# Five more projections with each hi weight tile run over hi and lo of the operand in one product

## The chip, the cores and the metric

The kernel runs on one core of a Trainium2 chip. The metric is the time of one execution on the device, in microseconds; of several runs the median counts. TensorE, the matrix engine, multiplies a stationary tile of weights (128x128) with a moving operand and adds into PSUM, which has eight banks of 128 partitions by 512 float32 columns. ScalarE (ACT) and VectorE (DVE) are the elementwise engines; both read PSUM. Weights come from HBM by DMA.

## The reference, cut to what matters

Two blocks on x with 256 tokens and 2048 features, batch 1, float32.

```python
# first block: RG-LRU
proj = rmsnorm(x, norm_pre) @ a_w_in            # 2048 -> 2 x 2048: xb and gate
xc   = causal_conv4(xb) + b;  r, i = sigmoid(blockwise(xc))
h    = scan(a(r), sqrt(1 - a^2) * i * xc);  y = (h * silu(gate)) @ a_w_out
x    = x + rmsnorm(y);  x = x + sigmoid(x @ ple_w_gate) * (p @ ple_w_proj)
# second block: one input projection, three branches
h = rmsnorm(x, g0)
u_pool, u_conv, c_gate, b_gate, q, k, v, q_idx, k_idx, w_idx = split(h @ w_in)
y_pool = (window_mean(u_pool) - u_pool) @ pool_w         # four window widths
y_conv = b_gate * causal_conv3(c_gate * u_conv)
y_attn = softmax over the 64 keys with the best index score (q_idx, k_idx, w_idx)
x = x + rmsnorm((sum of sigmoid(h @ w_gate) * (y @ w_branch)) @ w_out)
x = x + rmsnorm(square(relu(rmsnorm(x) @ w_up)) @ w_down)
```

The products are wanted to float32 accuracy. The kernel writes each operand as hi + lo, hi being rounded to 12 significant bits, and adds hi\*hi + hi\*lo + lo\*hi.

## The kernel before

**Layout and stream.** Features lie on the partitions and tokens on the free axis, so a product is a 128x128 tile of weights against 256 columns of the operand. All weights pass once, in the order of their use, through one stream (class `Stream`): a DMA on SP's queue brings a chunk (three buffers), ACT rounds it to hi (L88), DVE subtracts to lo (L99), in pieces of up to 1024 columns, that is, eight weight tiles (six in the conv projection). Five pieces are split ahead. `pumped` (L395), called after the products of each piece, emits the split of a later piece, whose buffer is that of the piece just multiplied; so on ACT each rounding waits until TensorE is done with that piece, and what is emitted behind it on ACT waits as well.

**Two forms of product.** `Group` (L344) holds four output tiles in two PSUM banks and makes three products of 256 columns per weight tile (L358): hi over the operand's hi, hi over its lo, lo over its hi. `Wide` (L367) gives each output tile a whole bank. The hi weights run once over 512 columns, hi and lo of the operand side by side (L378), into the two halves of the bank; the lo weights run over 256 columns into the left half (L379). The halves must be added at the evacuation: `merged` (L382) copies the right halves to SBUF on ACT (L387), one instruction per tile, and adds the left halves on DVE (L391), one per tile, and then the banks are free. Before the change `Wide` serves the ple gate, the branch gates, two branch products, most of w_out, and the MLP.

**The order beside the products** is set by `Sched`. A task (engine, cost in us, what it depends on, buffers it takes and frees) waits in one list, in order of creation. At each `pump`, once per piece, the list is walked in that order, and a task is emitted if its engine has room, its dependencies were emitted earlier (by at least one piece if on another engine, three for a TensorE task), and its buffers are free. DVE's room grows per eight-tile piece by 8 x 0.3275 - 1.13 = 1.49 us. Engines execute in order of emission. `make_room` (L165) is the way out when a new group needs banks that are not free: it takes the first task in the list that frees a bank and emits it at once, with all that it depends on, whatever the room. Freed banks are handed out again in the order in which they were freed. Large SBUF tiles of 128x4x256 are tagged T4, with ten buffers.

**Where the changed projections stand.** Block 1 runs, for m = 0 to 3, an xb group and a gate group of a_in (16 k-tiles by 4 tiles each), and between them, for m from 1 on, the recurrence gates `ri` of an earlier m: two `Group`s of one piece each. The sums of the first norm (`rstd`, L524) are wanted by every evacuation of a_in and are made during m = 1: a bank, tiny products (L532), a root on ACT (L545), five small DVE steps, a transposing product (L559). Then come a_w_out (three `Group`s open together) and the ple products. Block 2 projects key index, query index, key and query (`att_group`, 19 tiles), with v and the index weights (`vb`, two banks) after the third group; 16 index scores (`dots`, one bank each, L1020) run beside the query groups, the top-k on DVE (L1047) beside the first pool group, the relative bias goes through DRAM (L1085), then pool (two groups) and conv (eight groups of three tiles); attention's small products run beside the conv groups.

Of the kernel before, what the change touches and what calls it, by code (L numbers as in the profile page):

```python
"""RG-LRU block followed by a three-branch (pool / conv / sparse attention) block.

Everything on chip is laid out [feature on partitions, token on the free axis].
Every float32 product runs on the tensor engine as three float32r passes: an
operand v is split exactly into hi = round(v) (12 significant bits) and
lo = v - hi, and v*w = hi*hi + hi*lo + lo*hi.
"""
# [16 lines left out]
P = 128  # L24
T = 256
# [10 lines left out]
# columns of the packed per-feature vectors  # L36
# [12 lines left out]
class Stream:  # L49
    """The weights in the order of their use: loaded, split into hi and lo, handed out in pieces."""  # L50
# [28 lines left out]
    def split_hi(self):  # L79
        """Rounds one more piece; says how much of a full piece it was."""  # L80
        i = self.hi_done
        if i >= len(self.pieces):
            return 0.0
        _, _, w, src = self.piece(i)
        hi = self.pool.tile([P, 1024], F32R, tag="whi", bufs=self.hl_bufs, name=f"whi{i}")
        lo = self.pool.tile([P, 1024], F32R, tag="wlo", bufs=self.hl_bufs, name=f"wlo{i}")
        self.hl[i] = (hi[:, :w], lo[:, :w])
        self.nc.scalar.activation(hi[:, :w], src, AF.Copy)  # L88
        self.hi_done += 1
        return w / 1024  # L90

    def split_lo(self):
        """What the rounding of one more piece left."""
        i = self.lo_done
        if i >= self.hi_done:
            return 0.0
        c, last, w, src = self.piece(i)
        hi, lo = self.hl[i]
        self.nc.vector.tensor_tensor(lo, src, hi.bitcast(F32), op=ALU.subtract)  # L99
        self.lo_done += 1  # L100
        if last:
            del self.raw[c]
            self.load()
        return w / 1024
# [5 lines left out]
    def split_first(self, parts):  # L110
        """The first piece bit by bit, as it comes in."""
# [27 lines left out]
class Sched:  # L139
    """Spreads the work beside the matrix products over the pieces of the weight stream.  # L140

    A task is emitted once its engine has room in the current piece, the buffers that it takes
    are free, and what it depends on was emitted far enough ahead that no engine waits."""
# [3 lines left out]
    def __init__(self, bufs):  # L147
        self.q, self.now = [], 0
        self.room = {"ACT": 0.0, "DVE": 0.0, "POOL": 0.0, "PE": 0.0}
        self.left = dict(bufs)  # L150

# [13 lines left out]
    def make_room(self, **tags):  # L165
        """Emits tasks ahead of their turn until so many buffers are free."""
        for tag, n in tags.items():
            while self.left[tag] < n:
                self.need(next(t for t in self.q if tag in t.free))

    def emit(self, t):
        self.q.remove(t)
        self.make_room(**t.take)
        t.fn()
# [34 lines left out]
def tile_kernel(ctx: ExitStack, tc: tile.TileContext, d):  # L209
# [115 lines left out]
    def table(fn):  # L325
        """Brings the table of fn in before it is waited for."""
        act.activation(small(1, "tbl"), one, fn)
# [3 lines left out]
    # products of zeros keep TensorE at its full clock while it waits  # L331
# [12 lines left out]
    class Group:  # L344
        """Output tiles accumulated side by side, two to a PSUM bank."""
# [21 lines left out]
    class Wide:  # L367
        """Output tiles of one bank each: hi weights run over hi and lo of the operand side by side,
        into the two halves of the bank, which are added when the bank is evacuated."""
# [12 lines left out]
        def merged(self, box, name, *deps):  # L382
            """Tasks that leave the sum in box[name], a new tile."""
# [17 lines left out]
    def linear(grp, kts, rhs, pieces, last_kt, before=None):  # L401
        """Pieces of the stream, each [kt][tile] of 128 columns, into the group's tiles."""
# [22 lines left out]
    def full_by_bank(grp, rhs, evac, n=KT):  # L425
        """As full, but the first bank is finished, and evacuated, ahead of the second."""
# [26 lines left out]
    def q4(h, n):  # L453
        """hi and lo of four tiles"""
# [8 lines left out]
    def split_tasks(get, *deps, free=None):  # L463
        """get() -> hi, lo, source; the hi and lo of four tiles"""
# [10 lines left out]
    def scaled_tasks(h, k0, src, gname, *deps):  # L475
        """hi and lo of src * g, g per feature, for four tiles"""
# [12 lines left out]

    class Norm:  # L490
        """Sum of squares over the features and the reciprocal root of its mean."""
# [19 lines left out]
        def tasks(self, srcs, *deps):  # L511
            """Adds the squares of four tiles, in one or two parts."""
# [11 lines left out]
        def rstd(self, extra=(), wait=True, fill=(), idle=(0, 0)):  # L524
            """Tasks that leave in .r, [128, T], 1 / sqrt(mean + eps) in every partition, and by
            token in .c, [128, 2]; emitted at once where the next product waits for them."""
# [55 lines left out]
    # =====================================================================  # L582
    # block 1: RG-LRU
    # =====================================================================
# [24 lines left out]
    # softplus(-lam) = max(-lam, 0) + log1p(exp(-|lam|)),  log1p(e) = 2 atanh(e / (2 + e))  # L609
# [39 lines left out]

    def xb_done(m, grp):  # L650
        box = {}

        def scale():
            box["xb"], box["xc"] = t4(n="xb"), t4(n="xc")
            scale_banks(box["xb"], grp, n0.r)
# [18 lines left out]
        sc = Dv(1.2, scale, r_done[0], take=T4[2], free=PS[2])  # L674
# [5 lines left out]
    def g_done(m, grp):  # L680
        box = {}

        def scale():
            box["g"] = t4(n="g")
            scale_banks(box["g"], grp, n0.r)
# [8 lines left out]
        box["done"] = Dv(1.13, silu, A(0.95, sig, Dv(1.2, scale, r_done[0], take=T4[1], free=PS[2]), take=T4[1]),  # L694
# [3 lines left out]
    def ri(m):  # L698
# [19 lines left out]
        # with L = 8 r softplus(-lam), t = tanh(L / 2), a = exp(-L):  # L718
        # 1 - a = (1 + a) t  and  1 - a^2 = (1 + a)^2 t
# [43 lines left out]
    for m in range(4):  # L763
        grp = Group(4)
# [14 lines left out]
        grp = Group(4)  # L779
# [20 lines left out]
    def out_last(rhs, fill=(None, None), idle=(0, 0)):  # L800
        """The last four tiles, which the next product waits for; fill: products meanwhile."""
# [41 lines left out]
    # per-layer embedding: p @ ple_w_proj meanwhile  # L843
# [26 lines left out]
    # x += y * rstd, and its hi and lo, four tiles at a time  # L870
# [58 lines left out]
    # =====================================================================  # L929
    # block 2  # L930
    # =====================================================================
# [26 lines left out]
    att_ready = {}  # L958

    def att_group(i0, n):  # L960
        g = Group(n)
# [5 lines left out]
        def evac(m):  # L967
            dve.tensor_tensor(att_dst(i0 + m), g.ps(m), n2.r, op=ALU.mult)

        for m in range(n):  # L970
            att_ready[i0 + m] = Dv(0.35, lambda m=m: evac(m), r2_done[0], take=T4[1],
                                   free=PS[(n + 1) // 2 if m == n - 1 else 0])
# [5 lines left out]
    # v and wi with the tokens on partitions  # L978
# [26 lines left out]
    v_ready = A(0.9, v_done, att_ready[9], take=T4[1])  # L1005
    wi_ready = Dv(0.3, wi_done, v_ready, free=PS[2])

# [56 lines left out]
    # relative bias as a Toeplitz band: query q, key k reads rel[h, 127 - q + k].  One copy of rel  # L1064
    # per query lies in DRAM; reading it with a pitch one short of a copy shifts it by one per query.
# [149 lines left out]
    YS = hl16("YS")          # pool branch in tiles 0..7, conv branch in tiles 8..15  # L1215
    dhl, d_ready = {}, {}

    def pool_done(grp, n):
        box = {}

        def scale():
            box["u"], box["s"], box["q"] = t4(n="pu"), t4(n="pws"), t4(n="pq")
            scale_banks(box["u"], grp, n2.r)
# [24 lines left out]
        s = Dv(1.2, scale, take=T4[3], free=PS[2])  # L1248
# [4 lines left out]
    for n in range(2):  # L1253
        g = Group(4)
# [35 lines left out]
    def conv_done(m, grp):  # L1290
        box = {}

        def scale():
            box["uc"], box["z"] = t2(n="uc"), t1("z")
            dve.tensor_tensor(box["uc"], grp.banks[0], bc(n2.r, 2), op=ALU.mult)
            dve.tensor_tensor(box["z"], box["uc"][:, 0, :], box["uc"][:, 1, :], op=ALU.mult)
            S.free(T2=1)
# [12 lines left out]
        def gate():  # L1310
            dve.tensor_tensor(box["z"], grp.ps(2), n2.r, op=ALU.mult)
            dve.tensor_tensor(box["y"], box["y"], box["z"], op=ALU.mult)
# [7 lines left out]
        z = Dv(1.0, scale, take=dict(T2=1, T1=1))  # L1320
        y = Dv(0.8, taps, A(0.4, tap2, z, take=dict(T1=1)))
        y = Dv(0.7, gate, y, free=dict(ps=2, T1=1))
# [3 lines left out]
    for m in range(8):  # L1326
        g = Group(3)
# [215 lines left out]

def _kchunks(w, groups, kper=4):
    """w [K, M] -> [group, K / (kper * 128)][128][kper * len(group) * 128]: groups of column tiles."""
# [13 lines left out]
def _featT(a):  # L1559
    """[tokens, F] -> [128, F / 128, tokens]"""  # L1560
# [15 lines left out]
def _pack(i):  # L1576
# [15 lines left out]
    ri = np.concatenate([i["a_w_r"][0], i["a_w_i"][0]], axis=2)          # [8, 256, 512]  # L1592
# [3 lines left out]
    w = i["ple_w_proj"][0].reshape(2, P, 2, 2, 512).transpose(2, 1, 3, 0, 4)   # [chunk, p, grp, kt, 512]  # L1596
# [50 lines left out]
```

## Time and profile before

| | |
|---|---|
| median of 3 runs | 2001.24 us (1999.24, 2001.24, 2011.94) |
| span of the profiled execution | 2012.2 us |
| TensorE busy | 1984.8 us (99%), 13097 products |
| weight loads of TensorE | 1811.0 us (90%) |
| VectorE busy | 1274.3 us (63%) |
| ScalarE busy | 1001.4 us (50%) |
| DMA | 366 MB, 182 GB/s on average |
| chain that ended last | TensorE 96%: L378 40%, L358 33%, L379 20% |

A busy time on TensorE is the union of overlapping records: one 256-column product is recorded as 0.28 us, but the next one starts long before it ends. What a product costs the stream is the distance from its start to the next start.

### The profile page before, as it was taken

How to read it: one execution, taken by the hardware profiler on the slowest of the kernel's cores; microseconds unless marked ns; L12 is line 12 of the kernel's file. 1: busy time of each engine (PE TensorE's matmuls, PEld its weight loads, DVE VectorE, ACT ScalarE, POOL GpSimd, SP SyncE). 2: the span in 40 equal slices, each digit the busy share in tenths (PEclk: the TensorE clock that was granted, in tenths of full speed). 3: DMA queues.
4: the chain of work that ended last, by engine and by line, in shares of the span. 5: the costliest groups of instructions: out<-in, count | busy, mean ns of one | idle time of the engine just before them, and what ended most of it. 6: DMA issues, size and time to landing. Idle time of an engine off the chain costs nothing.

```text
span 2012.2 us, 31390 instructions
## 1 busy us (share of the span) xinstructions
PE 1984.8 (99%) x13097; PEld 1811.0 (90%) x13097; DVE 1274.3 (63%) x1642; ACT 1001.4 (50%) x1317; POOL 0.3 (0%) x6
## 2 busy tenths in 40 slices
PE   9999999999999999999999999999999999999996
PEld 8999999899999998888889989788888888888886
DVE  6788857765577776565656555865555556555665
ACT  6576755653434445454544455554444345434552
POOL 0000000000000000000000000000000000000000
PEclk9999999999999999999999999999999999999998
DMA  7545454554356455555555555455555555555552
GB/s 279 178 177 187 173 206 175 188 189 172 131 157 205 159 196 190 184 183 184 185 187 187 189 189 189 147 183 184 184 185 188 187 189 188 189 187 183 184 181 82
DMA packets 55846, 366.12 MB, mean 182 GB/s; under 512 B 6008, under 2 KB 8344, under 8 KB 16280
## 3 DMA queue, kind: packets, MB, share of 16 engines
q1 hardware_dynamic: 53424, 361.18, 51.6%
q10 hardware_dynamic: 2280, 2.93, 0.8%
q8 instruction: 102, 1.67, 0.3%
q14 instruction: 40, 0.33, 0.0%
HBM read 360.42 MB, written 3.67 MB: 181 GB/s over the span
## 4 chain that ended last, share of the span: by engine, by line
PE 96%; DVE 2%; DMA 1%; ACT 0%; issue 0%; SPq 0%; DVEq 0%; ACTq 0%
PE ps L378 40%; PE ps L358 33%; PE ps L379 20%; DMA wraw<-in_conv_in 1%; PE ps L1020 0%; DVE wlo L99 0%; DMA wraw<-in_a_in 0%; PE ps L1117 0%; DVE m L1529 0%; PE ps L532 0%; DVE X L1538 0%; PE ps L989 0%; PE ps L990 0%; PE ps L991 0%; DVE X L826 0%
## 5 line engine op out<-in xcount | busy, mean ns | idle before, releaser
L99 DVE TENSOR_TENSOR wlo<-wraw,whi 128x1024 fp32r<-128x1024 f32 (+2 forms) x701 | 831.1, 1190 | 663.3 <-ACT whi L88 662.4
L88 ACT ACTIVATE whi<-wraw 128x1024 fp32r<-128x1024 f32 (+2 forms) x701 | 721.6, 1032 | 934.8 <-PE ps L378 613.6
L378 PE MATMUL ps<-N,whi 128*128 128x512 f32 x1024 | 363.9, 400 | 3.5 <-DVE N L472 3.5
L378 PE MATMUL ps<-HD,whi 128*128 128x512 f32 x960 | 339.4, 399 | 0.0
L358 PE MATMUL ps<-G,whi 128*128 128x256 f32 x1632 | 300.2, 286 | 0.2 <-ACT whi L88 0.2
L379 PE MATMUL ps<-N,wlo 128*128 128x256 f32 x1024 | 288.2, 281 | 0.0
L378 PE MATMUL ps<-G,whi 128*128 128x512 f32 x768 | 271.0, 397 | 0.0
L379 PE MATMUL ps<-HD,wlo 128*128 128x256 f32 x960 | 269.6, 281 | 0.0
L358 PEld LDWEIGHTS ps<-G,whi 128*128 128x128 f32 x1632 | 256.4, 193 | 3.0 <-issue 0.6
L378 PEld LDWEIGHTS ps<-N,whi 128*128 128x128 f32 x1024 | 193.1, 189 | 52.6 <-DVE N L472 3.0
L358 PE MATMUL ps<-G,wlo 128*128 128x256 f32 x816 | 232.2, 285 | 3.4 <-DVE wlo L99 3.4
L378 PEld LDWEIGHTS ps<-HD,whi 128*128 128x128 f32 x960 | 180.4, 188 | 45.1
L379 PE MATMUL ps<-G,wlo 128*128 128x256 f32 x768 | 215.6, 281 | 0.0
L379 PEld LDWEIGHTS ps<-N,wlo 128*128 128x128 f32 x1024 | 194.2, 190 | 0.0
L358 PE MATMUL ps<-U,whi 128*128 128x256 f32 x1024 | 187.9, 286 | 1.8 <-ACT whi L118 1.6
L379 PEld LDWEIGHTS ps<-HD,wlo 128*128 128x128 f32 x960 | 181.3, 189 | 0.0
L378 PEld LDWEIGHTS ps<-G,whi 128*128 128x128 f32 x768 | 144.2, 188 | 35.2
L358 PEld LDWEIGHTS ps<-U,whi 128*128 128x128 f32 x1024 | 161.8, 194 | 3.2 <-ACT whi L118 2.2
L358 PEld LDWEIGHTS ps<-G,wlo 128*128 128x128 f32 x816 | 157.7, 193 | 3.8 <-DVE wlo L99 3.8
L358 PE MATMUL ps<-U,wlo 128*128 128x256 f32 x512 | 146.2, 286 | 0.2 <-DVE wlo L119 0.2
L379 PEld LDWEIGHTS ps<-G,wlo 128*128 128x128 f32 x768 | 145.1, 189 | 0.0
L358 PEld LDWEIGHTS ps<-U,wlo 128*128 128x128 f32 x512 | 99.4, 194 | 0.4 <-DVE wlo L119 0.4
(257 smaller groups left out, 2412.7 us busy)
## 6 DMA issues: line engine op xcount, KB each, us to landing
wraw<-in_up SPq DMA_DIRECT2D x64, 1024.0 KB, 4.8
wraw<-in_down SPq DMA_DIRECT2D x64, 1024.0 KB, 4.8
wraw<-in_gate SPq DMA_DIRECT2D x48, 1024.0 KB, 4.7
wraw<-in_a_in SPq DMA_DIRECT2D x29, 1024.0 KB, 4.8
wraw<-in_conv_in SPq DMA_DIRECT2D x32, 768.0 KB, 4.4
wraw<-in_branch SPq DMA_DIRECT2D x24, 1024.0 KB, 4.8
wraw<-in_a_out SPq DMA_DIRECT2D x16, 1024.0 KB, 4.8
wraw<-in_ple_gate SPq DMA_DIRECT2D x16, 1024.0 KB, 4.8
```

Of the source, the lines that this page charges most:

```text
L88: self.nc.scalar.activation(hi[:, :w], src, AF.Copy)
L99: self.nc.vector.tensor_tensor(lo, src, hi.bitcast(F32), op=ALU.subtract)
L358: pe.matmul(self.ps(m), lhsT, rhs, start=b not in self.begun, stop=stop, skip_group_check=True)
L378: pe.matmul(self.banks[m], wh, xhl, start=m not in self.begun, stop=False, skip_group_check=True)
L379: pe.matmul(self.banks[m][:, 0, :], wl, xhl[:, 0, :], start=False, stop=stop, skip_group_check=True)
```

## The change

The groups of a_in other than the first two, all `att_group`s, the pool groups and the conv groups become `Wide`. Their evacuations read the merged sum in SBUF and scale it there. In the att groups each tile has its own three tasks (copy, add, scale). The conv evacuation takes its tile from T4 in place of T2 and scales three tiles at once. `make_room` now skips tasks that wait for a task which is itself being emitted. All else in the diff is comments taken out.

```diff
     def make_room(self, **tags):
         for tag, n in tags.items():
             while self.left[tag] < n:
-                self.need(next(t for t in self.q if tag in t.free))
+                self.need(next(t for t in self.q if t.free.get(tag, 0) > 0 and self.clear(t)))
+
+    def clear(self, t):
+        return all(x.done is not None or (x not in self.busy and self.clear(x)) for x in t.deps)
...
+    def scale_tiles(box, name, grp, r):
+        if isinstance(grp, Wide):
+            dve.tensor_tensor(box[name], box[name], bc(r, 4), op=ALU.mult)
+        else:
+            box[name] = t4(n=name)
+            scale_banks(box[name], grp, r)
...
+    def scale_task(grp, box, name, scale, more):
+        if isinstance(grp, Wide):
+            return Dv(1.2, scale, r_done[0], grp.merged(box, name), take=T4[more])
+        return Dv(1.2, scale, r_done[0], take=T4[1 + more], free=PS[2])
...
-        sc = Dv(1.2, scale, r_done[0], take=T4[2], free=PS[2])
+        sc = scale_task(grp, box, "xb", scale, 1)
...
     for m in range(4):
-        grp = Group(4)
+        grp = Wide(4) if m else Group(4)
         if m == 0:
             grp_g = Group(4)
...
         if m > 1:
             ri(m - 1)
-        grp = Group(4)
+        grp = Wide(4)
         full(grp, rhsU)
         g_done(m, grp)
...
     def att_group(i0, n):
-        g = Group(n)
+        g = Wide(n)
         full(g, rhsG)
...
-        def evac(m):
-            dve.tensor_tensor(att_dst(i0 + m), g.ps(m), n2.r, op=ALU.mult)
+        def right(m):
+            act.activation(att_dst(i0 + m), g.banks[m][:, 1, :], AF.Copy)
+
+        def left(m):
+            dve.tensor_tensor(att_dst(i0 + m), att_dst(i0 + m), g.banks[m][:, 0, :], op=ALU.add)
+
+        def scale(m):
+            dve.tensor_tensor(att_dst(i0 + m), att_dst(i0 + m), n2.r, op=ALU.mult)
 
         for m in range(n):
-            att_ready[i0 + m] = Dv(0.35, lambda m=m: evac(m), r2_done[0], take=T4[1],
-                                   free=PS[(n + 1) // 2 if m == n - 1 else 0])
+            l = Dv(0.35, lambda m=m: left(m), A(0.4, lambda m=m: right(m), take=T4[1 if i0 + m in NEW else 0]),
+                   free=PS[1])
+            att_ready[i0 + m] = Dv(0.3, lambda m=m: scale(m), l, r2_done[0])
...
-        s = Dv(1.2, scale, take=T4[3], free=PS[2])
+        s = Dv(1.2, scale, grp.merged(box, "u"), take=T4[2])
...
     for n in range(2):
-        g = Group(4)
+        g = Wide(4)
         full(g, rhsG)
         pool_done(g, n)
...
-            dve.tensor_tensor(box["uc"], grp.banks[0], bc(n2.r, 2), op=ALU.mult)
+            dve.tensor_tensor(box["uc"][:, :3, :], box["uc"][:, :3, :], bc(n2.r, 3), op=ALU.mult)
...
-        z = Dv(1.0, scale, take=dict(T2=1, T1=1))
+        z = Dv(1.2, scale, grp.merged(box, "uc"), take=dict(T1=1))
         y = Dv(0.8, taps, A(0.4, tap2, z, take=dict(T1=1)))
-        y = Dv(0.7, gate, y, free=dict(ps=2, T1=1))
+        y = Dv(0.35, gate, y, free=dict(T4=1, T1=1))
...
     for m in range(8):
-        g = Group(3)
+        g = Wide(3)
         full(g, rhsG)
```

## Rows read from the trace of the kernel before

**Rows 1.** Busy times by stretch: length, PE, PEld, DVE, ACT, POOL, PEclk, DMA, GB/s
```profile
56.00:312.00 256.00, 256.00 (x2139) 256.00 (x2138) 193.28 (x245) 166.05 (x223) 0.00 (x0) 1.00 0.52 183
550.00:596.00 46.00, 46.00 (x380) 45.22 (x379) 38.34 (x89) 17.57 (x19) 0.00 (x0) 1.00 0.52 156
596.00:760.00 164.00, 160.44 (x1292) 159.00 (x1291) 119.05 (x196) 74.98 (x114) 0.00 (x0) 0.98 0.55 179
```

**Rows 2.** What PE waited for: us in total, times, longest us
```profile
PE ps L378 <- DVE N L472: 3.5, 2, 2.4
```

**Rows 3.** Timeline of PE in block 1, form of three products: start, us
```profile
199.85 0.40 PE L358 MATMUL ps<-U,whi 128*128 128x256 f32 x2
...
200.21 0.40 PE L358 MATMUL ps<-U,whi 128*128 128x256 f32 x2
```

**Rows 4.** Timeline of PE in the branch gates, wide form over G
```profile
999.83 0.40 PE L378 MATMUL ps<-G,whi 128*128 128x512 f32 x1
...
1000.89 0.40 PE L378 MATMUL ps<-G,whi 128*128 128x512 f32 x1
```

**Rows 5.** Timeline of PE in the ple gate, wide form over H
```profile
369.67 0.39 PE L378 MATMUL ps<-H,whi 128*128 128x512 f32 x1
...
371.75 0.39 PE L378 MATMUL ps<-H,whi 128*128 128x512 f32 x1
```

**Rows 6.** Timeline of ACT: in brackets the idle time before, and its releaser
```profile
71.77 1.06 ACT L88 ACTIVATE whi<-wraw 128x1024 fp32r<-128x1024 f32 x1 [1.82 <-PE ps L358]
...
514.70 0.84 ACT L88 ACTIVATE whi<-wraw 128x768 fp32r<-128x768 f32 x1 [2.68 <-PE ps L358]
515.45 0.47 ACT L1027 ACTIVATE rl<-ps 128x384 f32<-128x384 f32 x1
```

**Rows 7.** Groups by line and form: count, busy us, mean ns, idle before
```profile
L387 ACT ACTIVATE ms<-ps 128x256 f32<-128x256 f32 x64 | 19.0, 382 | 0.0
L391 DVE TENSOR_TENSOR ms<-ms,ps 128x256 f32<-128x256 f32 x64 | 22.5, 413 | 0.0
L709 ACT ACTIVATE r<-ps,vec 128x256 f32<-128x256 f32 x16 | 7.7, 481 | 0.0
L709 ACT ACT_TABLE_LOAD x2 | 2.6, 1283 | 0.0
L488 DVE TENSOR_TENSOR xb<-ps,R 128x512 f32<-128x512 f32 x8 | 5.1, 682 | 0.0
L1352 DVE TENSOR_TENSOR ms<-ms,R 128x1024 f32<-128x1024 f32 x12 | 14.7, 1225 | 0.4
L1158 ACT ACTIVATE p<-ps 128x512 f32<-128x512 f32 x4 | 2.1, 586 | 0.0
```

**Rows 8.** Chain that ended last, a norm's root to its transposing product: start, us
```profile
1261.15 0.27 ACT w L545
...
1262.32 0.45 PE ps L559 x2
```

**Rows 9.** Timeline of PE: the first norm's sums, during m = 1
```profile
59.73 0.50 PE L532 MATMUL ps<-one,nacc 128*128 128x1 f32 x4
```

**Rows 10.** Timeline of DVE: end of top-k and masks, then the pool's evacuation
```profile
571.00 0.42 DVE L1047 MAX8 m<-sc 128x8 f32<-128x256 f32 x1
...
572.39 0.28 DVE L1043 TENSOR_TENSOR sc<-sc,cst 128x128 f32<-128x128 f32 x1
...
576.49 0.68 DVE L488 TENSOR_TENSOR pu<-ps,R 128x512 f32<-128x512 f32 x1
```

**Rows 11.** Timeline of ACT's queue: the relative bias goes to DRAM
```profile
584.94 0.53 ACTq L1085 DMA_DIRECT2D relscr<-rs  x1
```

**Rows 12.** Busy times by stretch, columns as in rows 1
```profile
605.00:622.00 17.00, 13.44 (x87) 12.83 (x86) 13.55 (x27) 6.78 (x9) 0.00 (x0) 0.80 0.64 176
...
610.00:612.00 2.00, 0.18 (x2) 0.00 (x0) 1.90 (x6) 1.04 (x3) 0.00 (x0) 1.00 0.45 65
612.00:618.00 6.00, 4.93 (x23) 4.93 (x24) 5.86 (x13) 0.63 (x1) 0.00 (x0) 0.52 0.67 132
```

More of the change, by code (lines that the diff above doesn't have):

```diff
@@ L150, in __init__ @@
         self.left = dict(bufs)
+        self.busy = []
     def add(self, eng, cost, fn, *deps, take=None, free=None):
@@ L168, in make_room @@
             while self.left[tag] < n:
-                self.need(next(t for t in self.q if tag in t.free))
+                self.need(next(t for t in self.q if t.free.get(tag, 0) > 0 and self.clear(t)))
+    def clear(self, t):
+        return all(x.done is not None or (x not in self.busy and self.clear(x)) for x in t.deps)
     def emit(self, t):
         self.q.remove(t)
+        self.busy.append(t)
         self.make_room(**t.take)
+        self.busy.remove(t)
         t.fn()
@@ L653, in scale @@
         def scale():
-            box["xb"], box["xc"] = t4(n="xb"), t4(n="xc")
-            scale_banks(box["xb"], grp, n0.r)
+            box["xc"] = t4(n="xc")
+            scale_tiles(box, "xb", grp, n0.r)
         def tap3(i):
@@ L683, in scale @@
         def scale():
-            box["g"] = t4(n="g")
-            scale_banks(box["g"], grp, n0.r)
+            scale_tiles(box, "g", grp, n0.r)
         def sig():
@@ L692, in silu @@
             dve.tensor_tensor(box["g"], box["g"], box["s"], op=ALU.mult)
-        box["done"] = Dv(1.13, silu, A(0.95, sig, Dv(1.2, scale, r_done[0], take=T4[1], free=PS[2]), take=T4[1]),
+        box["done"] = Dv(1.13, silu, A(0.95, sig, scale_task(grp, box, "g", scale, 0), take=T4[1]),
                          free=T4[1])
@@ L958, in tile_kernel @@
     att_ready = {}
+    NEW = (1, 5, 9, 11, 15)
     def att_group(i0, n):
-        g = Group(n)
+        g = Wide(n)
         full(g, rhsG)
@@ L1003, in wi_done @@
                               op0=ALU.mult, op1=ALU.mult)
-    v_ready = A(0.9, v_done, att_ready[9], take=T4[1])
+    v_ready = A(0.9, v_done, att_ready[9])
     wi_ready = Dv(0.3, wi_done, v_ready, free=PS[2])
@@ L1221, in scale @@
         def scale():
-            box["u"], box["s"], box["q"] = t4(n="pu"), t4(n="pws"), t4(n="pq")
-            scale_banks(box["u"], grp, n2.r)
+            box["s"], box["q"] = t4(n="pws"), t4(n="pq")
+            scale_tiles(box, "u", grp, n2.r)
         def window(half):
@@ L1293, in scale @@
         def scale():
-            box["uc"], box["z"] = t2(n="uc"), t1("z")
-            dve.tensor_tensor(box["uc"], grp.banks[0], bc(n2.r, 2), op=ALU.mult)
+            box["z"] = t1("z")
+            dve.tensor_tensor(box["uc"][:, :3, :], box["uc"][:, :3, :], bc(n2.r, 3), op=ALU.mult)
             dve.tensor_tensor(box["z"], box["uc"][:, 0, :], box["uc"][:, 1, :], op=ALU.mult)
-            S.free(T2=1)
         def tap2():
@@ L1310, in gate @@
         def gate():
-            dve.tensor_tensor(box["z"], grp.ps(2), n2.r, op=ALU.mult)
-            dve.tensor_tensor(box["y"], box["y"], box["z"], op=ALU.mult)
+            dve.tensor_tensor(box["y"], box["y"], box["uc"][:, 2, :], op=ALU.mult)
         def hi():
```

## The prediction

> **What bounds the kernel now.** I read the page first: TensorE is busy for 99% of the span and makes up 96% of the chain that ended last, so nearly every microsecond is a matter of how products follow one another. The busy times by stretch say the same of the parts that change: in block 1 DVE is busy for 75% and ACT for 65%, in the conv part DVE for 73%, while over the pool groups, where the top-k runs, DVE reaches 83% [rows 1]. Then the waits of TensorE: the longest kind adds up to 3.5 us [rows 2], so no wait is there to be removed. A gain can come only from cheaper products, and a loss only from waits that are not there now.
>
> **The products.** Three products of 256 columns take 0.36 us per weight tile, start to start [rows 3]. The wide form takes (1000.89 - 999.83)/3 = 0.353 us over G [rows 4], which att, pool and conv read, and (371.75 - 369.67)/6 = 0.347 us over H [rows 5]. Tiles that change form: a_in 6 groups x 64 = 384, att 19 x 16 = 304, pool 2 x 64 = 128, conv 8 x 48 = 384, together 1200. The saving is 1200 x 0.0067 = 8.0 us by the row of G, 16 us by the row of H. I take 8.0: G is the operand itself for 816 of the tiles, and U, the operand of the rest, has no wide row. The weights and their order in the DMA queue stay as they are.
>
> The Trainium skill, page "TensorE: Matmul & The Clock Gate", section "Wait — 56ns, not 53.3ns?", has a product start to start at its columns over 2.4 GHz and a fixed 2.5 ns or so. By it, joining two products of 256 columns saves one fixed part, so 3.0 us over 1200 tiles, an estimate from that page, and the sum below would end 5 us higher. Both forms in this trace are slower than the page has them, and the measured difference is nearer to 7 ns, so the rows decide.
>
> **Work added beside the products.** 75 output tiles (24 + 19 + 8 + 24) get a copy on ACT, 19.0/64 = 0.30 us each, and an add on DVE, 22.5/64 = 0.35 us each [rows 7]: 22 us on ACT, 26 us on DVE. The scaling costs about what it did: one pass of 1.22 us in SBUF for two of 0.68 us from PSUM [rows 7]; the 19 att tiles get one more pass. In block 1 that lifts DVE from 75% to about 79%. This work is hidden under the products as long as its result is not wanted at once, so I cost it at nothing; what it costs where the cover is missing are the waits that follow. T4 buffers stand as before, since the merged tile takes the place of the scaled one; only conv takes a T4 where it took a T2.
>
> **Waits that the change adds.** All have one root: a wide group holds four of the eight banks, not two, and its successor another four. A product that waits for a bank holds up all products behind it.
>
> A. The first norm. During m = 1 the xb and gate groups of m = 0 still hold four banks, since their scaling needs the norm; the wide xb group holds the other four. The norm's sums, made today in passing at 59.7 us [rows 9], need a bank. None is free until `make_room` forces one for the next group. It forces the copy that ends the norm, and before the sums' bank the merge of the group just finished. TensorE then stands through a chain: rounding of the next piece 1.06 us, which can't start earlier because ACT waits for TensorE's release [rows 6], four copies 1.19, a table load 1.28 [rows 7] for the root, root to transposing product 1262.77 - 1261.15 = 1.62 us [rows 8]. Sum 5.2 us. After an idle stretch of 2 us the granted clock stood at about half (1.2 GHz) for 6 us, worth 2.9 us of products [rows 12]; I add 2.0. A = 7.2; bounds 3.9 (no table load, no fall of the clock) and 8.1.
>
> B. Four places in block 1 have the two `ri` groups between the last wide group and the next: 4 + 2 + 2 banks, so the next group starts in banks that are not evacuated. The first freed are those of the first `ri` group: rounding 1.06 and three sigmoids of 0.48 [rows 6, 7] give 2.5 us, and 3.8 where the sigmoid table has to be loaded. If the merge of the wide group frees first, nothing waits, since that group ended two pieces earlier. DVE has spare room only before the third place, so I take 2.5 at three and 0.5 there: B = 8.0, bounds 0 and 2 x 2.5 + 2 x 3.8 = 12.6.
>
> C. While the last att group runs, its three banks, four of the group before it and one index score make eight. Each further score waits for the previous one's evacuation: rounding 0.84 + relu 0.47 = 1.3 us [rows 6], twice until the adds come: 2.6; bounds 0 and 5.2.
>
> D. The second pool group finds one bank free, because the att adds stand behind the top-k in the list. `make_room` forces the relative bias's way to DRAM and the three adds, which on DVE come after the last round and the masks: 572.67 - 571.00 = 1.7 [rows 10] + 0.41 [rows 7] = 2.1 us; bounds 1.1 and 4.
>
> E. In the conv part two groups leave two banks, and attention wants four for its transpositions. The second pair waits rounding 0.84 + copy 0.59 = 1.4 us [rows 6, 7], the score products about as much, so up to 6 us for both kv heads; half of the time conv's banks will have come free: 3.0, bounds 0 and 6.
>
> F. A stall that exists: the bias write leaves at 584.94 [rows 11], weights come late, and from 605 to 622 us 87 products were made where 17/0.12 = 142 fit, a loss of 6.5 us [rows 12]. By D the write leaves some 10 us earlier, with larger pieces in stock: -2.0, bounds -6.5 and +3.
>
> **Sum.** -8.0 + 7.2 + 8.0 + 2.6 + 2.1 + 3.0 - 2.0 = +12.9 us. The profiled span of 2012.2 us would become 2025; it is 11 us longer than the median of the runs (2001.2), so I put the difference on the median: 2014.1 us. With all bounds: -17.5 to +30.9.
>
> **Rivals.** (1) The queues come in time: B, C and E near nothing, F -4, A without the clock: -8.0 + 5.2 + 2.1 - 4.0 = -4.7, so 1996.5 us. For it: ACT and DVE idle a fifth of the time or more. Against it: in B and C the evacuation sits behind a rounding that waits for TensorE itself, so idle time doesn't help. (2) Slower: forced attention. When a conv group finds fewer than three banks, `make_room` takes the first task in the list that frees one, and attention's come before conv's; with it goes the chain behind it. A block of queries is some five DVE passes of 1.2 us and four exponentials of 0.48 (sized by rows 7), 8 us; both blocks forced add 16 us, so 2030 us. It decides if conv's adds don't get DVE within the eight pieces of the next group. For it: attention's tasks stand first in each pump, and conv's DVE work grows by about 1.1 us per group. Against it: DVE is at 73% there [rows 1], and the adds free banks earlier than the old gate did. (3) The saving is that of H, 16 us, with waits as in (1): 1988 us; U and G don't show it. (4) The page's saving of 3.0 us with the waits as forecast: 2019 us.
>
> **How the numbers follow.** Forecast 0.42 (its own range 2004 to 2024), (1) 0.25, (2) 0.25, (3) 0.03, (4) 0.05. About 1% (20 us) is what a measurement can tell from no change. Slower by more holds (2) and the forecast's upper end, 0.30; faster by more holds only what of (3) lies below 1981, 0.03; the rest, 0.67, is within. 1990 to 2033 leaves out (3), the lower end of (1) and the upper half of (2).
>
> **What would show it.** Right: products at 0.353 us per tile over G; a gap on TensorE of 5 us near 80 us, ended by L559; gaps of 2 to 3 us after `ri`, ended by L709, L710 or the adds; L1085 issued before the second pool group. Wrong: no gaps in block 1 (A or B fails), 0.347 us over U, or gaps over 5 us in conv, ended by attention's tasks.

## The result and the profile after

| | before | after |
|---|---|---|
| median of 7 runs each, side by side | 2000.53 us (1998.12 to 2011.94) | 2019.95 us (2006.41 to 2025.62) |
| ratio after / before, 95% interval | | 1.0075 [1.0048, 1.0103] |
| span of the profiled execution | 2012.2 us | 2011.3 us |
| first a_in product to first a_w_out product | 212.0 us | 232.1 us |
| a_w_out, 256 tiles in three products | 105.0 us | 107.1 us |
| first att product to first product of the branches (att, v, pool, conv, first gate) | 370.6 us | 360.8 us |
| one quarter of the MLP up or down, 256 wide tiles | 90.45 us | 88.75 us |
| TensorE busy | 1984.8 us, 13097 products | 1965.9 us, 11897 products |

The change costs about 15 us by the ratio (0.75% of 2000 us; 10 to 21 by its interval); 12.9 was forecast. The two spans can't be subtracted: the last but one line of the table is code that the change does not touch, and there the two executions differ by 13 us (1984 wide tiles in the MLP at 0.353 or 0.347 us). Runs of both kernels lie in two groups some 12 us apart, about this difference (before, one of 7 runs is in the higher group; after, four of 7), so the medians, 19.4 us apart, overstate the change, and the comparison goes by stretches of the traces.

By stretches: block 1 lost 20.1 us in a_in and 2.1 in a_w_out, 22.2 us; block 2's changed part gained 9.8 us; together the kernel after is 12.4 us slower.

What TensorE waited for in the kernel after (the view of waits; total us, times, longest). Before, the longest kind was 3.5 us [rows 2]:

```profile
PE ps L385 <- DVE N L479: 5.0, 3, 2.4
PE ps L574 <- DVE c L569: 4.3, 3, 2.5
PE ps L365 <- DVE mg L398: 4.2, 1, 4.2
PE ps L385 <- DVE mxb L398: 4.2, 1, 4.2
PE ps L385 <- ACT r L728: 2.1, 1, 2.1
PE ps L547 <- DVE mxb L398: 1.8, 1, 1.8
PE ps L385 <- DVE al L468: 1.2, 1, 1.2
PE ps L1047 <- ACT rl L1054: 1.2, 1, 1.2
...
PE ps L365 <- DVE xcl L468: 1.2, 1, 1.2
...
PE ps L385 <- DVE qT L991: 0.8, 1, 0.8
```

(L365 is the three-product form, L385 and L386 the wide form, L394 and L398 the copy and the add of `merged`.) The same waits in order of time, from the timeline of TensorE; in brackets the idle time and what ended it:

```profile
81.02 0.58 PE L547 MATMUL ps<-one,nacc 128*128 128x1 f32 x4 [1.85 <-DVE mxb L398]
84.14 0.69 PE L574 MATMUL ps<-cst,c 128*128 128x128 f32 x2 [2.54 <-DVE c L569]
...
118.26 0.50 PE L385 MATMUL ps<-U,whi 128*128 128x512 f32 x1 [2.12 <-ACT r L728]
...
119.86 0.77 PE L385 MATMUL ps<-U,whi 128*128 128x512 f32 x1 [0.62 <-DVE mg L398]
...
153.00 0.47 PE L385 MATMUL ps<-U,whi 128*128 128x512 f32 x1 [4.18 <-DVE mxb L398]
...
237.96 0.77 PE L365 MATMUL ps<-Y,whi 128*128 128x256 f32 x2 [4.23 <-DVE mg L398]
```

The first pair is the first norm, forced (step A). The others stand behind the gate products `ri` (step B): after ri(0), ri(1) and ri(3) TensorE waits for banks. With the wait of 1.2 us for the gates' operand (xcl, at 110.3) these are 16.7 us of idle time. Behind each of the four places shown, part of the next 5 to 10 us runs at the lower of the two clock levels (1.2 in place of 2.4 GHz), so that the mean granted clock (PEclk) is below 1. Busy times by stretch (length, PE, PEld, DVE, ACT, POOL, PEclk, DMA, GB/s):

```profile
84.50:90.00 5.50, 5.50 (x21) 4.73 (x20) 3.95 (x6) 0.47 (x1) 0.00 (x0) 0.58 0.00 0
...
119.90:126.00 6.10, 6.10 (x27) 5.26 (x28) 3.21 (x6) 2.37 (x4) 0.00 (x0) 0.73 0.34 144
...
153.00:158.00 5.00, 5.00 (x19) 4.25 (x20) 4.34 (x6) 2.78 (x6) 0.00 (x0) 0.66 0.61 210
238.00:248.00 10.00, 10.00 (x66) 10.00 (x67) 6.86 (x9) 6.82 (x12) 0.00 (x0) 0.77 0.46 146
```

TensorE is fully busy in each of them, but 21 products (10.5 tiles) in 5.5 us are 3.7 us of work at 0.353 us a tile. The losses are 1.8, 1.3 and 1.6 us in the first three; a_w_out, which has no wait inside, takes 2.1 us more than before: nearly 7 us. Idle time and slow products are 23.5 us. Less 2.6 us for the cheaper products (384 x 0.0067; somewhat more, since part of a_in runs at 0.347 us a tile, see below) this leaves up to 21 of the 22.2 us.

Why the banks came so late is seen on DVE and ACT behind ri(1), the third wait (timelines; the copies `mxb<-ps` are the ACT line):

```profile
146.71 2.43 DVE L756 TENSOR_TENSOR_SCAN s<-a,i 128x256 f32<-128x256 f32 x4
149.06 1.20 DVE L99 TENSOR_TENSOR wlo<-wraw,whi 128x1024 fp32r<-128x1024 f32 x1
150.17 1.22 DVE L774 TENSOR_TENSOR s<-s,g 128x1024 f32<-128x1024 f32 x1
151.31 1.21 DVE L99 TENSOR_TENSOR wlo<-wraw,whi 128x1024 fp32r<-128x1024 f32 x1
152.44 1.07 DVE L398 TENSOR_TENSOR mxb<-mxb,ps 128x256 f32<-128x256 f32 x3
```

```profile
146.86 1.19 ACT L394 ACTIVATE mxb<-ps 128x256 f32<-128x256 f32 x4
```

The copies are done at 148.1. The adds that free the banks come on DVE only at 152.4, behind a scan, a product and two weight splits. DVE is not idle in between: it has a backlog, and the merge stands at its end.

In block 2 the waits are short. The timeline of TensorE in the kernel after shows four: an index score (C), the second pool group (D), late weights (F) and the first product that wants attention's result:

```profile
549.52 0.48 PE L1047 MATMUL ps<-kiT,qi 64*128 64x256 f32 x1 [1.20 <-ACT rl L1054]
...
594.29 0.47 PE L385 MATMUL ps<-G,whi 128*128 128x512 f32 x1 [0.80 <-DVE qT L991]
...
632.95 0.39 PE L386 MATMUL ps<-G,wlo 128*128 128x256 f32 x1 [0.68 <-DVE wlo L99]
...
774.42 0.50 PE L385 MATMUL ps<-G,whi 128*128 128x512 f32 x1 [1.23 <-DVE al L468]
```

The granted clock over 435 to 796 us is 1.00 throughout. Of the stall of before near 612 us [rows 12] the wait of 0.7 us above is the longest that is left. Products in the kernel after, twice over U and twice over G, three tiles from line to line:

```profile
100.20 0.39 PE L385 MATMUL ps<-U,whi 128*128 128x512 f32 x1
...
101.24 0.39 PE L385 MATMUL ps<-U,whi 128*128 128x512 f32 x1
...
196.29 0.40 PE L385 MATMUL ps<-U,whi 128*128 128x512 f32 x1
...
197.35 0.40 PE L385 MATMUL ps<-U,whi 128*128 128x512 f32 x1
...
660.08 0.39 PE L385 MATMUL ps<-G,whi 128*128 128x512 f32 x1
...
661.12 0.39 PE L385 MATMUL ps<-G,whi 128*128 128x512 f32 x1
...
690.33 0.40 PE L385 MATMUL ps<-G,whi 128*128 128x512 f32 x1
...
691.39 0.40 PE L385 MATMUL ps<-G,whi 128*128 128x512 f32 x1
```

That is 0.347 and then 0.353 us a tile over U, and 0.347 and then 0.353 over G. The two rates are those that G and H had before [rows 4, rows 5], but here each operand has both, so the operand does not decide the rate.

### The profile page after: what moved, and what is told of

It is laid out like the page before. It is cut to its first block, busy times and chain, and to the rows that moved or that the text cites. A ratio compares the mean times of both kernels' runs of the same rounds, so it can differ in the third digit from the quotient of the medians.

```text
span 2011.3 us, 29156 instructions
## 1 busy us (share of the span) xinstructions
PE 1965.9 (98%) x11897; PEld 1746.1 (87%) x11897; DVE 1297.1 (64%) x1701; ACT 1024.2 (51%) x1394; POOL 0.3 (0%) x6
## 4 chain that ended last, share of the span: by engine, by line
PE 93%; DVE 4%; DMA 1%; ACT 1%; issue 1%; SPq 0%; DVEq 0%; ACTq 0%
PE ps L385 52%; PE ps L386 27%; PE ps L365 12%; DMA wraw<-in_conv_in 1%; DVE wlo L99 1%; PE ps L1047 0%; ACT whi L88 0%; DMA wraw<-in_a_in 0%; PE ps L1144 0%; DVE m L1554 0%; DVE X L845 0%; PE ps L547 0%; DVE s L756 0%; DVE xc L687 0%; DVE X L1563 0%
## 5 line engine op out<-in xcount | busy, mean ns | idle before, releaser
L385 PE MATMUL ps<-G,whi 128*128 128x512 f32 x1584 | 561.1, 398 | 2.0 <-DVE al L468 1.2
L386 PE MATMUL ps<-G,wlo 128*128 128x256 f32 x1584 | 444.3, 280 | 1.2 <-DVE wlo L99 1.2
L385 PEld LDWEIGHTS ps<-G,whi 128*128 128x128 f32 x1584 | 297.2, 188 | 74.5 <-DVE al L468 1.6
L385 PE MATMUL ps<-N,whi 128*128 128x512 f32 x1024 | 356.3, 392 | 5.0 <-DVE N L479 5.0
L385 PE MATMUL ps<-HD,whi 128*128 128x512 f32 x960 | 333.0, 391 | 0.0
L386 PEld LDWEIGHTS ps<-G,wlo 128*128 128x128 f32 x1584 | 299.1, 189 | 2.3 <-DVE wlo L99 2.1
L386 PE MATMUL ps<-N,wlo 128*128 128x256 f32 x1024 | 286.7, 280 | 0.0
L386 PE MATMUL ps<-HD,wlo 128*128 128x256 f32 x960 | 268.8, 280 | 0.0
L385 PEld LDWEIGHTS ps<-N,whi 128*128 128x128 f32 x1024 | 191.6, 187 | 48.3 <-DVE N L479 4.5
L385 PEld LDWEIGHTS ps<-HD,whi 128*128 128x128 f32 x960 | 179.5, 187 | 39.4
L386 PEld LDWEIGHTS ps<-N,wlo 128*128 128x128 f32 x1024 | 193.5, 189 | 0.0
L386 PEld LDWEIGHTS ps<-HD,wlo 128*128 128x128 f32 x960 | 181.4, 189 | 0.0
L385 PE MATMUL ps<-U,whi 128*128 128x512 f32 x384 | 140.1, 408 | 6.9 <-DVE mxb L398 4.2
L386 PE MATMUL ps<-U,wlo 128*128 128x256 f32 x384 | 109.6, 285 | 0.0
L365 PE MATMUL ps<-Y,whi 128*128 128x256 f32 x512 | 94.3, 287 | 4.2 <-DVE mg L398 4.2
L385 PEld LDWEIGHTS ps<-U,whi 128*128 128x128 f32 x384 | 74.7, 194 | 25.6 <-issue 5.3
L385 PE MATMUL ps<-YS,whi 128*128 128x512 f32 x256 | 90.9, 399 | 0.0
L385 PE MATMUL ps<-H,whi 128*128 128x512 f32 x256 | 89.2, 392 | 0.7 <-ACT yg L813 0.6
L365 PEld LDWEIGHTS ps<-Y,whi 128*128 128x128 f32 x512 | 81.6, 196 | 4.4 <-issue 4.4
L386 PEld LDWEIGHTS ps<-U,wlo 128*128 128x128 f32 x384 | 74.8, 195 | 0.0
```

What stands on the lines that cost most here:

```text
L365: pe.matmul(self.ps(m), lhsT, rhs, start=b not in self.begun, stop=stop, skip_group_check=True)
L385: pe.matmul(self.banks[m], wh, xhl, start=m not in self.begun, stop=False, skip_group_check=True)
L386: pe.matmul(self.banks[m][:, 0, :], wl, xhl[:, 0, :], start=False, stop=stop, skip_group_check=True)
```

## Experiments

The bank theory: TensorE waits for banks in block 1, and that alone is the loss; block 2 gains. Its rivals: the added copies and adds cost wherever they are (51 of the 75 tiles lie in block 2), or the order has no part in it and all is the spread of the MLP.

The stretches of all kernels, in us, run between the first starts of products over U, Y, H, G and YS (the trace by operand): a_in from U to Y, a_w_out from Y to H, att to conv from G to YS. Start-up varies a_in by up to 1.5 us between executions: its first two groups, the same 384 products in all kernels, take 49.6 to 51.2 us. Each ratio is against the kernel before, run beside it.

| kernel | a_in | a_w_out | att to conv | median | ratio, 95% interval |
|---|---|---|---|---|---|
| before | 212.0 | 105.0 | 370.6 | 2000.5 | |
| after | 232.1 | 107.1 | 360.8 | 2020.0 | 1.0075 [1.0048, 1.0103] |
| 1 block 2 only | 212.2 | 105.0 | 361.6 | 1991.8 | 0.9950 [0.9932, 0.9968] |
| 2 block 1 only | 231.2 | 107.5 | 370.8 | 2024.0 | 1.0125 [1.0098, 1.0153] |
| 3 norm's bank free | 221.4 | 107.7 | 362.9 | 2001.5 | 1.0013 [0.9990, 1.0037] |
| 4 merge ahead | 217.6 | 105.0 | 360.7 | 1997.8 | 0.9976 [0.9953, 0.9999] |
| 5 both mended | 209.9 | 105.0 | 360.6 | 1988.6 | 0.9934 [0.9912, 0.9956] |
| 6 before, bias early | 211.5 | 105.0 | 365.0 | 1997.5 | 0.9971 [0.9948, 0.9994] |
| 7 all mended | 209.5 | 105.1 | 361.8 | 1990.8 | 0.9937 [0.9915, 0.9959] |
| 8 banks only | 215.3 | 106.4 | 360.6 | 1998.9 | 0.9972 [0.9944, 0.9999] |
| 9 all mended, bias early | 209.3 | 105.0 | 359.2 | 1999.8 | 0.9948 [0.9918, 0.9978] |

**1 and 2: one block alone.** In 1, a_in keeps the three products; in 2, att, pool and conv do.

```diff
-        grp = Wide(4) if m else Group(4)
+        grp = Group(4)
...
-        grp = Wide(4)
+        grp = Group(4)
         full(grp, rhsU)
         g_done(m, grp)
```

> Only block 2's projections (att, pool, conv) take the wide form; a_in is left in three products as before the change. Bank theory: all of the loss is TensorE waiting for banks in block 1 (its a_in stretch grew from 212.0 to 232.1 us, with half clock behind each wait), and block 2 gains some 10 us. Then this kernel is about 10 us faster than before, near 1990 us, its a_in stretch is 212 us again, and the stretch from the first att product to the end of the conv part is 360 to 362 us as in the changed kernel. Rival, work: the added copies and adds (51 of the 75 tiles are in block 2) cost everywhere; then this kernel is slower than before by about two thirds of the loss, some 10 us, near 2010 us. Rival, spread: nothing in the order matters and the difference is which of two product rates (0.347 or 0.353 us per wide tile) an execution falls in; then it is the same as both within 5 us.

> Only a_in's six groups take the wide form, block 2 is as before the change. Bank theory: the loss of block 1 stands alone, 20 us in a_in and 2 us at the half clock behind it, so about 2022 us against 2000 before, with the waits of 2.4 to 4.5 us at the same four places. Rival, work: 24 of the 75 tiles, so a third of the loss, some 5 us, near 2005 us. If the gain of block 2 comes from the earlier write of the relative bias, the loss of 6 us near 605 to 622 us is back here, since the write is late again.

Both came out as the bank theory has it. Against the runs of before beside them (median 2001.4) block 2 alone is 9.6 us faster and block 1 alone 22.6 us slower, with nearly the same waits (2.1, 3.8 and 3.9 us behind `ri`). The rival of the spread falls, since the stretches ahead of the MLP show loss and gain. The rival of the work falls in its general form: two thirds of the copies and adds lie in block 2, and it got faster; what they cost in block 1 is the matter of kernel 8. And the late weights of step F are back in 2, as long as before (kernel before, then kernel 2):

```profile
613.07 0.58 PE L358 MATMUL ps<-G,wlo 128*128 128x256 f32 x1 [2.89 <-DVE wlo L99]
```

```profile
636.14 0.58 PE L365 MATMUL ps<-G,wlo 128*128 128x256 f32 x1 [2.89 <-DVE wlo L99]
```

**3: step A alone undone.**

```diff
-        grp = Wide(4) if m else Group(4)
+        grp = Wide(4) if m > 1 else Group(4)
```

> As the changed kernel, but the xb group of m = 1 is in three products, so that two banks stay free for the first norm (it also gives up the wide saving of 64 tiles, 0.4 us). Forecast of step A: the two gaps between 78.9 and 84.1 us (4.9 us) and the half clock behind them go, 7 us of the changed kernel's time, near 2010 us by the median, a_in 225 us. If the waits of step B come from DVE's backlog that the forced norm left behind, they shrink too and a_in falls to 218 us or less; if they come from banks of their own, the gaps of 2.4, 4.5 and 4.5 us stand.

a_in fell by 10.7 us, to 221.4, between the two values that had been named (225 and 218). That is more than A's idle time of 4.4 and its half clock of 1.8 us: the wait for xcl went too, and the next two gaps, start to start, shrank from 2.4 (with a second one of 0.9 behind it) to 1.3 us and from 4.5 to 3.5 us; the last stayed at 4.5. So A also left a backlog that cost the waits behind it some 4 us. The waits that remain do not come from A.

**4: step B alone mended.** The merge of the last wide group is emitted at the head of `ri`, ahead of its products:

```diff
-    def ri(m):
+    def ri(m, wide):
...
         S.need(xb["done"])
+        S.need(wide.merge)
```

> As the changed kernel, but the copies and adds that free the four banks of the last wide group are emitted ahead of the recurrence gates' products, in place of behind their sigmoids and the recurrence's work. Nothing is computed otherwise. Order theory: the next group's banks are free after 5.8 us of gate products, so the gaps at 116, 148 and 233 us (2.4, 4.5 and 4.5 us) go with the half clock behind them: a_in 232 falls to about 216 to 220 us and the whole to some 2005 us by the median. Rival, capacity: ACT and DVE have too much to do here in whatever order; then the waits move to the gate products (operand of the gates late) and the time stays within 4 us of the changed kernel.

a_in fell by 14.5 us, a_w_out is back at 105.0. Of the waits at the three places behind `ri` one is left, of 0.7 us. The adds now begin 0.5 us behind the last gate product (143.08 us), not 3.9 (152.44 against 148.54) as in the kernel after (DVE, then TensorE):

```profile
143.60 1.39 DVE L398 TENSOR_TENSOR mxb<-mxb,ps 128x256 f32<-128x256 f32 x4
```

```profile
144.05 0.50 PE L385 MATMUL ps<-U,whi 128*128 128x512 f32 x1 [0.69 <-DVE mxb L398]
```

Nothing is computed less. The rival of capacity falls: it was the place of the merge in the queue.

**5: both edits.**

> The changed kernel with both edits that were tried alone: the xb group of m = 1 in three products (step A), and the merge of the last wide group ahead of the gate products (step B). Bank theory: no wait is left in block 1, so a_in falls below the 212.0 us of before by the wide saving of its five remaining wide groups (320 tiles at 0.007 to 0.013 us, 2 to 4 us): 208 to 210 us; the whole 1987 to 1990 us, 2 to 4 us less than with the wide form in block 2 alone (1991.8). Rival, capacity: with waits gone TensorE runs faster into ACT's and DVE's work and new waits of 2 us or more come up in block 1; then a_in stays at 212 us or above and the whole is no better than 1992 us.

a_in takes 209.9 us, 2.1 less than before: 320 tiles at 0.0066 us each, and there is no wait of block 1 left behind the start-up. This is a version that beats both kernels: 12 us faster than before, by the medians (9 to 18 by the interval) as by the stretches, and 24.5 us faster than the kernel after by the stretches (31 by the medians, which were not taken side by side). How little room there is, the busy times of this kernel from the first wide product to a_w_out show:

```profile
79.90:216.00 136.10, 135.95 (x836) 121.10 (x835) 122.28 (x158) 104.10 (x153) 0.00 (x0) 1.00 0.53 185
```

DVE is busy for 122.3 of 136.1 us, 90%.

**6: step F alone, in the kernel before.**

```diff
     for n in range(2):
+        if n == 1:
+            S.need(rel_ready)
         g = Group(4)
         full(g, rhsG)
```

> The kernel before with one edit: the relative bias's way to DRAM is emitted ahead of the second pool group, as the bank shortage does in the changed kernel. Nothing is wide that was not. Theory of step F: the late weights near 605 to 622 us come from this write; some 10 us earlier it meets a larger stock of weights, and the gap of 3.2 us and the half clock behind it shrink by 2 to 6.5 us: the stretch from the first att product to the end of conv 364 to 368 us in place of 370.6. Rival: the stall moves with the write and keeps its size (370 us), and the whole gain of block 2 is cheaper products.

The write left 161.7 us after the first att product in place of 171.2, and the stretch takes 5.6 us less with nothing wide that was not. A wait of 0.9 us is left of 2.9, and the granted clock stays at 1.00:

```profile
609.02 0.39 PE L358 MATMUL ps<-G,wlo 128*128 128x256 f32 x1 [0.90 <-DVE wlo L99]
```

```profile
609.00:616.00 7.00, 6.98 (x57) 6.87 (x57) 6.83 (x14) 2.82 (x4) 0.00 (x0) 1.00 0.72 238
```

So 5.6 us, more than half of block 2's gain of 9.8, can be had without the wide form: in the kernel after, the shortage of banks forced a DMA to a better time.

**7: steps C and D mended on top of 5.** The merges of the last two att groups are emitted at the end of their products:

```diff
+        if i0 > 8:
+            S.need(*ls)
```

> As the kernel with both edits in block 1, and the copies and adds of the last two att groups emitted as soon as their products are, in place of behind the index scores. Steps C and D: the waits of 1.5 us (index scores) and 1.3 us (second pool group, for its banks) go, together 2 to 3 us of block 2's 361 us; the top-k then starts a little later. Rival: DVE, which runs the index sums at that time, gives the wait back to the scores or the masks, and attention ends later at the gates (a wait of 1.5 us there now): 361 us and the time of the kernel with both edits, within 1.5 us.

Both waits went, and the stretch is no shorter (361.8 against 360.6). Nothing forces the bias's way to DRAM any more; the write leaves 169.6 us after the first att product, and the late weights are back, with the slow products behind them:

```profile
606.10 0.49 PE L385 MATMUL ps<-G,whi 128*128 128x512 f32 x1 [1.35 <-ACT whi L88]
607.10 0.58 PE L386 MATMUL ps<-G,wlo 128*128 128x256 f32 x1 [0.50 <-DVE wlo L99]
```

```profile
607.00:612.00 5.00, 4.72 (x16) 3.84 (x17) 4.86 (x12) 3.16 (x4) 0.00 (x0) 0.66 0.47 116
```

The rival had foreseen no gain, but for another reason: what the two waits gave was lost again to late weights, while attention's end kept its wait of 1.3 us.

**9: the same with the write forced early** (the edit of 6).

> The kernel with all four places mended, and the relative bias's way to DRAM emitted ahead of the second pool group. With the merges of the att groups early, nothing forced that way any more, and the write left 169.6 us after the first att product, in place of 158.7 in the kernel with block 1's two edits; two waits for weights, 1.6 and 1.0 us, stood near 606 us. Theory: the waits of C and D did go, and step F gave them back; with the early write as well, the waits near 606 us shrink to 1 us or less together and the stretch from the first att product to the end of conv is 358 to 360 us (361.8 without, 360.6 with block 1's edits alone). Rival: the forced write brings DVE's backlog back to the second pool group, which waits 1 us or more, and the stretch stays at 360.5 us or above.

The write left 157.8 us after the first att product, and one wait of 0.7 us for weights is left. The stretch is 359.2 us, the shortest of all: 2.6 less than without the edit, 1.4 less than 5. The median, 1999.8, does not show it: the profiled execution of 9 takes 90.45 us for a quarter of the MLP and that of 7 takes 88.75, which is 13 us in code that is the same in both. At this size the stretch decides, not the median, and as a whole kernel 9 is not shown to beat 5.

**8: the banks without the work.** In five groups of block 1 three products per tile again, but each output tile in a bank of its own; no copies, no adds:

```diff
+    class Spread(Group):
+        def ps(self, m):
+            return self.banks[m][:, 0, :]
...
-        grp = Wide(4) if m else Group(4)
+        grp = Spread(4) if m > 1 else Group(4)
```

> As the changed kernel in block 2. In block 1 the second gate group and the groups of m = 2 and 3 are in three products again, without a copy or an add, but each output tile holds a bank of its own, half of it unused: the banks of the wide form without its work; the xb group of m = 1 is in two banks. Bank theory: holding four banks is what costs, so TensorE waits at the same three places behind the gate products (with the first norm's banks free they were 1.3, 3.5 and 4.5 us), and a_in takes 218 to 224 us. Rival, work: the waits come from the copies and adds that stand in the way on ACT and DVE; without them a_in takes 212 to 214 us.

The result, 215.3 us, lies between the two theories. Two waits are left behind `ri`, where 3 has three (1.0, 3.2 and 4.2 us of idle time), and they are shorter:

```profile
137.39 0.47 PE L385 MATMUL ps<-U,whi 128*128 128x256 f32 x2 [0.75 <-DVE xb L511]
...
220.83 0.77 PE L365 MATMUL ps<-Y,whi 128*128 128x256 f32 x2 [2.70 <-DVE g L511]
```

Against before, the banks alone cost 3.3 us in a_in and 1.4 in a_w_out, 4.7 together; kernel 3, which has the same groups wide, lost 9.4 + 2.7 = 12.1 although its products are 2.1 us cheaper. That makes a third. But start-up took 1.4 us less in 8 than in 3; counted from the end of the first two groups it is 5.2 of 13.2 us, two fifths. The rest goes with the copies and adds in DVE's and ACT's queues at these places. So neither theory holds alone in block 1: the wide form takes the banks, and its merge frees them late.

## Why the prediction was right, and where it was not

The total was right by luck: two errors of 10 us cancelled. Forecast for block 1: A + B less 2.6, that is 12.6 us; it lost 22.2. Forecast for block 2: +0.3; it gained 9.8.

**The products**: right for block 1, with 0.0066 us a tile over U in kernel 5. In block 2, 9.8 us less the 5.6 of F, with 3.9 us of new gaps (1.4 each at the scores and at attention's end, 1.2 at the pool, start to start), leave some 8 us for 816 tiles, 0.010 a tile, between the rows of G and H. This is a remainder, not measured by itself; it fits the two rates, 0.347 and 0.353, that both occur in this stretch. The choice of the row of G because G is the operand had no ground: 0.347 us shows over U as well, which the prediction had named as a sign of being wrong. The fixed part of a product that the Trainium skill states (page "TensorE: Matmul & The Clock Gate", section "Wait — 56ns, not 53.3ns?"), 2.5 ns or so, does not agree: one product saved is worth 6.6 to 13 ns here.

**A**: right in place and mechanism, and in size (7.2; idle 4.4 and slow products 1.8). ACT's timeline behind the first two waits has the chain as it was forecast, rounding, copies and table load:

```profile
79.10 1.06 ACT L88 ACTIVATE whi<-wraw 128x1024 fp32r<-128x1024 f32 x1 [1.76 <-PE ps L385]
80.06 1.19 ACT L394 ACTIVATE mxb<-ps 128x256 f32<-128x256 f32 x4
81.68 1.28 ACT L560 ACT_TABLE_LOAD   x1 [0.44 <-PE ps L547]
```

What it missed is the backlog that the forced tasks leave on DVE, 4 us more in later waits.

**B**: the place was right, the size was not. It assumed that the wide group's merge would come in time or else that the sigmoids would free the banks after 2.5 us. Only the first wait is of that kind (2.1 us). At the others the merge did come first, but 4.2 us late, since its adds stood at the end of DVE's backlog. The step that failed is "If the merge of the wide group frees first, nothing waits, since that group ended two pieces earlier": it took the end of the group's products for the time at which DVE has come to the adds. And B counted no half clock behind its waits, which A did: 5.0 us more (1.3 and 1.6 in a_in, 2.1 in a_w_out). B measured some 16 us (11.2 idle, 5.0 of slow products) for 8.0 forecast; kernel 4 took 16.6 out of a_in and a_w_out. Its upper bound of 12.6 was too low as well.

**C, D and E**: too large. C came once and not twice, 1.2 us for 2.6. D was 0.8 us for 2.1. E did not come: attention's products waited for no bank in conv, and only its end was late, by 1.2 us at the first gate of the next part.

**F**: the mechanism was right and its size was not: 2.0 forecast, 5.6 measured in kernel 6. In the kernel after, the write left 158.8 us after the first att product (before, 171.2 [rows 11]), so the 10 us taken for it were about right. But they saved nearly all of the stall, its half clock included, which the prediction had only as its bound of 6.5. This also answers the prediction's sentence that no wait is there to be removed: the stall was one, and removing most of it gave these 5.6 us.

```profile
L1112 ACTq DMA_DIRECT2D relscr<-rs x1: 530/530/530, 594.1 to 594.1; - x1
```

**The rivals.** (1), the queues come in time, fell for block 1 and held for block 2. (2), attention forced in conv, is refuted by the trace: no gap over 1.1 us, start to start, from the first product of the second pool group to the end of conv. (3) had H's rate, which did show, in part, in both blocks; its waits were wrong for block 1. (4) had the wrong saving; that its 2019 us is the number nearest to the median of 2020.0 is chance, since the stretches moved by 12.4 us and not by 18.

## What to carry to other kernels

A form that holds twice the banks is paid where the group after the next wants them: follow each bank to the instruction that frees it and count what stands ahead of it in that engine's queue; when the group's products end does not tell it. Emitting the merge at the end of its products, ahead of the work behind it, was worth 14.5 us of 20 here, and no new wait came of it. When a shortage forces something early, look at what else comes forward with it: a DMA moved by 10 us gave 5.6 us, more than twice what the cheaper products gave in block 1 (2.1), and part of that went when the shortage was mended (2.6 us, which kernel 9 got back).

## What the runs showed of the hardware

**Two rates of one product stream.** The wide form runs at 0.347 or at 0.353 us a tile. In the MLP it stays at one of them for hundreds of microseconds; in a_in and in block 2 both occur in one trace over the same operand, as the lines above over U and G show. In these two traces the mean duration of a wide hi product over HD differs with the rate (groups by line; before, at 0.353, then after, at 0.347):

```profile
L378 PE MATMUL ps<-HD,whi 128*128 128x512 f32 x960 | 339.4, 399 | 0.0
```

```profile
L385 PE MATMUL ps<-HD,whi 128*128 128x512 f32 x960 | 333.0, 391 | 0.0
```

The same code with the same weights takes 90.45 or 88.75 us a full quarter of the MLP in every trace here, and the ple gate took 91.7 us in kernels 2, 3 and 7 and 90.2 elsewhere. Over the MLP's 1984 tiles that is 13 us. No experiment here was aimed at what picks the rate, and it stays open.

**The clock after a wait.** The granted clock was 1.00 behind single waits of 0.8 to 1.2 us in block 2, and on average 0.58 to 0.77 in the 5 to 10 us behind waits of 2.1 to 4.2 us, shown above; in kernel 7 it was 0.66 behind two waits, of 1.35 and 0.50 us, that lie 1.0 us apart. One of the first kind, behind attention's end (busy times by stretch, kernel after):

```profile
774.40:780.00 5.60, 5.58 (x31) 4.88 (x32) 4.46 (x8) 2.67 (x6) 0.00 (x0) 1.00 0.05 12
```

What the half clock cost is seen most cleanly in a_w_out, whose products are the same in all kernels: 105.0 or 105.1 us where no wait precedes it, 106.4 behind a wait of 2.7 us, 107.1 to 107.7 behind waits of 3.9 to 4.2 us.
